# A hybrid token mixer and MLP on one core: the rest of the modulation moved beside the delta rule's inverses

## The chip, the core and the metric

The kernel runs on one NeuronCore of a Trainium2 chip. A core has five engines that matter here, each with its own queue that it works off in order: TensorE (PE; its weight loads are shown apart as PEld), VectorE (DVE), ScalarE (ACT), GpSimd (POOL), and SyncE (SP), which here only issues DMA transfers. ACT and POOL issue some transfers too. Working memory is SBUF (128 partitions); matrix products land in PSUM, eight banks of 128 x 512 floats. The metric is the device time of the whole program in microseconds.

## The reference, cut to what matters

One layer: a token mixer (Hyena long convolution, gated linear attention "GLA", gated delta rule "GDN") and an MLP. Both take shift, scale and gate from a modulation vector, which is a product of SiLU(c), one row, with a matrix of 1024 x 6144.

```python
silu_c = jax.nn.silu(c)
silu_cc = jax.nn.silu(c_ctx)
sh1, sc1, g1, sh2, sc2, g2 = jnp.split((silu_c @ w_mod[l] + b_mod[l])[:, None, :], N_MOD, axis=-1)
csh1, csc1, cg1, csh2, csc2, cg2 = jnp.split(silu_cc @ w_mod[l] + b_mod[l], N_MOD, axis=-1)
h = modulate(x, norm1_g[l], sh1, sc1)
hc = modulate(ctx, norm1_g[l], csh1, csc1)
y, yc = mixer(h, hc, ...)
x = x + g1 * y
x = x + g2 * sq_relu_mlp(modulate(x, norm2_g[l], sh2, sc2), w_mlp1[l], w_mlp2[l])
return rmsnorm(x, final_norm_g)
```

`sh1` and `sc1` are needed before the first projection. The other four parts (`g1`, `sh2`, `sc2`, `g2`) are needed only after the mixer. There are 1024 latent tokens and 256 context tokens.

## The kernel before

The program is written as straight code; a scheduler then sets the order on each engine from the order of writing, from priorities and from its own estimate of times. That order is fixed when the program is built, and on the chip each engine takes its instructions in that order, whatever is ready. A tile belongs to a pool; when a pool is closed, its memory or its PSUM banks go to the next pool on the same side, whose first writer then waits for the last reader of what lay there.

The stages in order:

- Norm, Hyena filters and the first third of the modulation (`mod_group(0)`).
- Input projection: pieces of 128 channels, each 24 products of 128 x 512 per half of the tokens (tiles `psb<-ahi,wh`, `alo,wh`, `ahi,wl`; `ch`, `cl` for the context), weights through `ws`, `wh`, `wl`. Conv pieces are followed by taps on DVE (`acc<-psb,vecs,acc`). Beside the first of them runs the Hyena convolution (tiles `pss`, `hb`, `lv`, `wrh`, `wrl`, `dft`).
- `mod_rest` makes the other two thirds of the modulation. It is a generator; before the change two steps of it are written after each piece of `SEQ[0]`. One group of it (there are two) takes eight row blocks of `wmod`. A row block is 128 rows by 2048 columns of float32, fetched as two halves of 512 KB into the tile `mw` (two buffers). Each half feeds two products with `cs32` (32 columns) as the stationary side. The four products of a row block write four different quarters of 32 partitions of one PSUM bank, `psd`. At the end of a group, ACT copies the bank to SBUF (L452), PE transposes it in four pieces and DVE adds the bias into `modT`.
- `gdn_prep` makes the matrices of the delta rule for four heads (tiles `psp`, `dm`, `KQ`).
- `inverse` inverts triangular matrices for the delta rule: 15 substitution steps in blocks of 16 with the constant selector `sel` (1 MB in SBUF) as the stationary side, then products of 32 x 32 and of 64 x 64 blocks (all in `psi`). Two generators run in `rounds`; every fourth round one gate piece or one decay of `SEQ[2]` is written between.
- `gla_pair`, twice: seven levels of products `pss<-bd,lv` (the last two `bd,kT`), then states. `gdn_loops`: ten steps for four heads (tiles `psl`; a step reads `kv`, `kq`, `at`, its products are `psl<-S,kq`, `r,NT`, `vn,kv`, `vn,at`). The first reads `kv,NT`. `gdn_loops` and the pairs overlap.
- Output projection, MLP, final norm. These read `modT` again.

The pool `psm` (one bank) and the pool `mw` lie on the right side; so do `ia` (the inverse's SBUF, with `sel`), `psi`, and later `nl` and `psl` of `gdn_loops`.

Of the kernel before, what the change touches and what calls it, by code (L numbers as in the profile page):

```python
# [7 lines left out]
F32 = mybir.dt.float32  # L8
# [11 lines left out]
LC = L + CTX  # L20
# [165 lines left out]
EVERY = 4  # L186
ENG = {'eqf': 'vvvvvpvvvvppvv', 'eqr': 'vvvvvvvvvvvvvv', 'qh0': 'vvvvvvvvvvvvvv', 'qh1': 'pppppppppppppp', 'ekf': 'pppppppppppppp', 'ekr': 'vvpppppppppppp', 'kk': 'vvvvvvvvvpvvvv', 'qd0': 'aa', 'qd1': 'aa', 'A': 'vvaa', 'te': 'vvvv', 'ke': 'vvvv', 'kt': 'aaaa', 'A2': 'pppppppppppppppp', 'q2': 'vpvpvpvp', 'og': 'aaaaaaaa', 'ov': 'vv', 'mid': 'paa', 'pk': 'vvvv', 'pq': 'pvpp', 'tri': 'pppppppppppppppp', 'KQ': 'aaaaaaaaaaaaaaaaaaaa', 'C': 'avavavavavavavav', 'off': 'pppp', 'Y': 'pppp', 'T32': 'pppp', 'Ya': 'vvvvvvvvvvvvvvvvvvvvvvvvvvvvvv', 'V': 'aaaa', 'V64': 'aaaa', 'pu': 'aavvaavvaavvaavv', 'NT': 'avavavavavavavavavavavavavavavav', 'Yh': 'vvvvvvvvvvvvvvvv', 'V128': 'aaaaaaaa', 'sp1': 'pppppppppppppppp', 'sp0': 'vvvvvvvvvvvvvvvv', 'spc': 'vvvvvvvvvvvvvvvv', 'sps': 'vvvvvvvvvvvvvvvv', 'wl': 'vvvvvvvvvvvvvvvv', 'yg': 'vvvvvvvv', 'Sl': 'vvvvvvvvvvvvvvvv', 'ft': 'vvvvvvvvvvvvvvvv', 'oq': 'pvpp', 'qs': 'aaaaaaaa', 'S2': 'aaaaaaaa', 'pl': 'vvpvvpvv', 'xr': 'vpvvvvvv', 'kd': 'pppppppp', 'u': 'aaaa'}
ENGC = {'eqf': 'vp', 'eqr': 'vp', 'qh0': 'vp', 'qh1': 'vp', 'ekf': 'vp', 'ekr': 'vp', 'kk': 'vp', 'qd0': 'avp', 'qd1': 'avp', 'A': 'va', 'te': 'vp', 'ke': 'vp', 'kt': 'va', 'A2': 'pva', 'q2': 'vp', 'og': 'va', 'ov': 'vp', 'mid': 'pva', 'pk': 'vp', 'pq': 'vp', 'tri': 'vp', 'KQ': 'va', 'C': 'avp', 'off': 'vp', 'Y': 'pva', 'T32': 'pva', 'Ya': 'vp', 'V': 'va', 'V64': 'va', 'pu': 'va', 'NT': 'avp', 'Yh': 'avp', 'V128': 'va', 'sp1': 'vp', 'sp0': 'vp', 'spc': 'vp', 'sps': 'vp', 'wl': 'vp', 'yg': 'vp', 'Sl': 'vp', 'ft': 'vp', 'oq': 'vp', 'qs': 'av', 'S2': 'avp', 'pl': 'vp', 'xr': 'vp', 'kd': 'vp', 'u': 'av'}
SEQ = ('gk1 gv0 dk0 dq0 gk0 dk1 dv2 gv1 dq1 dk2 gq0 dq2', '0 1 2 dv0 gq1 3 dv1 gv2', 'dg1 0 gg1 gg0 dg0 3 1 gg2 2 dg2')
MODN = 2  # L190
FPOOL = ((0, 2, 5), (0, 2, 5))
# [20 lines left out]
class Build:  # L212
# [99 lines left out]
    def run(self):  # L312
        tc, nc = self.tc, self.nc
        self._cst, self.y, self.nT, self.nS, self.rooms = {}, [], 0, 0, {i: i - 9 for i in range(4)}
        with ExitStack() as es:
# [12 lines left out]
            def tp(name, bufs, right=False, **k):  # L328
                p = tc.tile_pool(reuse_waits="tile", name=name, bufs=bufs, side="right" if right else "left", **k)
                return p, p.__enter__()  # L330
# [23 lines left out]
            close(p0)  # L354
            h, mw = tp("hy", 1, True), tp("mw", 2, True)
            self.H = h[1]
            self.hyena()
            mods = self.mod_rest(psm[1], mw[1])
            piece = lambda n: (self.gdn_conv if n[0] == "d" else self.gla_piece)(n)
            for n_ in SEQ[0].split():  # L360
                piece(n_)
                for _ in range(MODN):
                    next(mods, None)
            for _ in mods:
                pass
            close(mw, h, psm, pss, lv)

# [9 lines left out]

            ia, ib, psi = tp("ia", 1, True), tp("ib", 1, True), ps("psi", 2, True)
            self.inverse_start(ia[1])
            dw = tp("dw", 1, True)  # L380
            dec = self.gla_decays(dw[1])
            rest = [dec[int(n)] if n.isdigit() else (lambda n=n: (self.gate_piece if n[1] == "g" else piece)(n)) for n in SEQ[2].split()]
            self.rounds([self.inverse([X[2 * i + j]["NT"] for j in range(2)], (ia, ib)[i][1], psi[1], f"psi{i}") for i in range(2)], rest, EVERY)
            close(psi, dw, ib, ia)
            close(psb, cv, w, act)
# [53 lines left out]
    def mod_group(self, g, psum, pname, wpool, wnames):  # L439

        nc = self.nc
        ps = psum.tile([128, 512], F32, name=pname)
        for kt in range(8):
            for hf in range(2):
                w = wpool.tile([128, 1024], F32, name=wnames[hf])
                nc.sync.dma_start(w, self.I["wmod"][g, kt, hf])
                for q2 in range(2):
                    q = 2 * hf + q2
                    self.mm(ps[32 * q:32 * q + 32, :], self.cs32[:, kt, :], w[:, 512 * q2:512 * q2 + 512], kt == 0, kt == 7)
            yield  # L450
        ms = wpool.tile([128, 1024], F32, name=wnames[0])[:, :512]
        nc.scalar.copy(ms, ps)  # L452
        pt = psum.tile([128, 512], F32, name=pname)
        for s in range(4):
            self.transpose(pt[:, 128 * s:128 * s + 128], ms[:, 128 * s:128 * s + 128])
        src = pt.rearrange("p (s q c) -> p s q c", s=4, q=4)
        o, _ = _VC["bmod"]
        for col in range(2 if g == 0 else 1):
            self.tt(self.modT[:, 16 * g:16 * g + 16, col].rearrange("p (q s) -> p s q", q=4), src[:, :, :, col],
                    self.vecs[:, o + 16 * g:o + 16 * g + 16].rearrange("p (q s) -> p s q", q=4), ADD)  # L460
        yield

    def mod_rest(self, psum, pool):

        for g in (1, 2):
            yield from self.mod_group(g, psum, "psd", pool, ("mw", "mw"))
        self.stt(self.A2, self.modT[:, 32:40, 0], 1.0, self.vec("n2"), ADD, MUL)
        for g in (20, 44):
            self.ts(self.modT[:, g:g + 4, 0], self.modT[:, g:g + 4, 0], -1.0, MUL)
        self.show("modT", self.modT)  # L470
        yield
# [257 lines left out]
    def gla_decays(self, P):  # L729

        nc, x = self.nc, {}
        wa2 = self.cs32.rearrange("p a b -> p (a b)").rearrange("p (a b) -> p a b", a=2)[:48]

        def start():
            nc.sync.dma_start(wa2, self.I["wa2"])
            ab, smask = x["ab"], x["smask"] = P.tile([48, LC], F32, name="ab"), P.tile([128, LC], F32, name="smask")
            for d in range(2):
                nc.sync.dma_start(ab[32 * d:32 * d + 16], self.dz["gk0"][48 + 64 * d:64 + 64 * d])
            nc.gpsimd.memset(smask, 1.0)
            nc.gpsimd.memset(smask.rearrange("p (a b) -> p a b", b=64)[:, :, 0:1], 0.0)  # L740

        def one(p, d):
# [12 lines left out]
            st = 1 - 2 * d  # L755
            nc.vector.tensor_tensor_scan(t[:, ::st], x["smask"], g[:, ::st], 0.0, op0=MUL, op1=ADD)
            nc.sync.dma_start(self.dcum[p][d], t)
# [289 lines left out]

    def rounds(self, gens, fill=(), every=1):

        n, fill = 0, list(fill)  # L1050
        while gens:
            gens = [g for g in gens if next(g, self) is not self]
            n += 1
            if fill and n % every == 0:
                fill.pop(0)()
        for f in fill:
            f()

    def gdn_loops(self, X):
# [743 lines left out]
```

## Time and profile before

| | |
|---|---|
| median of 3 runs | 1643.51 us (1642.14 to 1655.13) |
| the profiled execution | 1638.78 us |
| its span in the trace | 1637.0 us |
| PE busy | 1509.1 us, 92% of the span |
| DVE busy | 1236.8 us, 76% |
| ACT busy | 803.0 us, 49% |
| POOL busy | 694.8 us, 42% |

The trace is of one execution; 1.8 us of that execution lie outside the span. Times of the trace count from the start of the span. A busy share is an average over stages, so each stage is looked at by itself: the rows further down give stretches of the span, with what each engine did in them.

### The profile page before, as it was taken

Reading aid. Unit: us, or ns where it says so; the run is one execution under the profiler, and the core shown is the slowest. Engines: PE = TensorE matmul, PEld = TensorE weight load, DVE = VectorE, ACT = ScalarE, POOL = GpSimd, SP = SyncE. Lnnn points to the kernel's source line nnn. Section 1 sums busy time; section 2 is a strip of 40 time slices with the busy share of each in tenths; the row PEclk is TensorE's granted clock in tenths of the full one; section 3 lists DMA queues with packets and bytes.
Section 4 is the critical chain, followed back from the end, with each engine's and each line's share of the span. In section 5 each row is a group of like instructions: output and inputs, shape, how many; then the busy total and the mean of one; then the engine's idle time right before and its main releaser. Section 6 shows DMA issues by size and latency. Waiting matters only on the chain.

```text
span 1637.0 us, 26134 instructions
## 1 busy us (share of the span) xinstructions
PE 1509.1 (92%) x10096; PEld 1215.9 (74%) x10096; DVE 1236.8 (76%) x1827; ACT 803.0 (49%) x1462; POOL 694.8 (42%) x494
## 2 busy tenths in 40 slices
PE   7799999989899898758799799999999999999996
PEld 2378877767688676557788687788888888888886
DVE  5963589897576387688887978987679758974995
ACT  5432222315655644445565356654565456446553
POOL 0311141331434330154762354655556555655553
PEclk9899999999999997778889899999999999999998
DMA  8432777756566531136436934364454535453532
GB/s 296 135 110 90 248 258 273 230 188 203 161 211 201 164 135 46 66 118 185 139 112 208 306 103 105 102 155 129 105 140 116 155 83 150 103 142 94 133 70 104
DMA packets 114292, 248.42 MB, mean 152 GB/s; under 512 B 28919, under 2 KB 74407, under 8 KB 101240
## 3 DMA queue, kind: packets, MB, share of 16 engines
q1 hardware_dynamic: 85800, 167.03, 30.3%
q0 software_dynamic: 9808, 59.77, 16.3%
q10 hardware_dynamic: 18560, 19.94, 4.0%
q8 instruction: 80, 1.31, 0.3%
q14 instruction: 44, 0.36, 0.1%
HBM read 196.57 MB, written 41.75 MB: 146 GB/s over the span
## 4 chain that ended last, share of the span: by engine, by line
PE 62%; DVE 22%; ACT 5%; DMA 5%; issue 4%; POOL 2%; SPq 0%; POOLq 0%; ACTq 0%; DVEq 0%
PE psb L224 47%; PE pss L224 8%; DVE lv L252 4%; DVE T L252 3%; PE psl L224 2%; DVE ar L260 2%; DVE hb L252 2%; DVE ar L252 1%; PE psi L224 1%; PE psd L224 1%; DVE acc L260 1%; DVE bd L252 1%; DMA dft<-in_fw 1%; DVE psb L252 1%; DMA alo<-in_xT 1%
## 5 line engine op out<-in xcount | busy, mean ns | idle before, releaser
L224 PE MATMUL psb<-T,S 128*128 128x512 f32 (+1 forms) x3072 | 693.7, 387 | 6.7 <-DVE T L252 3.4
L224 PEld LDWEIGHTS psb<-T,S 128*128 128x128 f32 x3072 | 571.3, 189 | 127.6 <-DVE T L252 5.2
L252 POOL TENSOR_TENSOR S<-wr,S 128x512 fp32r<-128x512 f32 x252 | 366.3, 1468 | 303.4 <-ACT S L292 302.9
L292 ACT CAST S<-wr 128x512 fp32r<-128x512 f32 x252 | 155.0, 620 | 146.9 <-PE psb L224 106.5
L224 PE MATMUL psb<-ahi,wh 128*128 128x512 f32 x448 | 183.5, 411 | 8.5 <-ACT ahi L292 4.3
L224 PE MATMUL psb<-alo,wh 128*128 128x512 f32 x448 | 181.9, 406 | 0.0
L224 PE MATMUL psb<-ahi,wl 128*128 128x512 f32 x448 | 180.6, 403 | 0.0
L252 POOL TENSOR_TENSOR wl<-ws,wh 128x1024 fp32r<-128x1024 f32 x28 | 71.0, 2537 | 208.5 <-ACT wh L292 138.9
L260 DVE SCALAR_TENSOR_TENSOR acc<-psb,vecs,acc 128x504 f32<-128x504 f32 (+5 forms) x168 | 111.2, 677 | 50.4 <-ACT acc L264 48.1
L260 DVE SCALAR_TENSOR_TENSOR x<-psb,modT,x 128x512 f32<-128x512 f32 (+1 forms) x148 | 105.2, 727 | 40.4 <-PE psb L224 40.0
L252 DVE TENSOR_TENSOR T<-h,T 128x512 fp32r<-128x512 f32 x88 | 86.2, 1010 | 46.1 <-ACT T L292 44.8
L224 PEld LDWEIGHTS psb<-ahi,wh 128*128 128x128 f32 x448 | 87.1, 195 | 39.6 <-issue 9.1
L252 DVE TENSOR_TENSOR T<-ar,T 128x512 fp32r<-128x512 f32 x112 | 111.7, 1024 | 6.2 <-ACT T L292 5.9
L224 PEld LDWEIGHTS psb<-alo,wh 128*128 128x128 f32 x448 | 87.1, 195 | 25.7 <-issue 8.0
L224 PEld LDWEIGHTS psb<-ahi,wl 128*128 128x128 f32 x448 | 87.1, 194 | 22.3 <-issue 5.1
L292 ACT CAST T<-ar 128x512 fp32r<-128x512 f32 x112 | 68.5, 620 | 43.8 <-DVE ar L260 29.3
L252 POOL TENSOR_TENSOR bd<-lv,qT 64x1024 f32<-64x1024 f32 x16 | 49.2, 3082 | 37.3 <-PE pss L224 25.1
L264 ACT ACTIVATE acc<-psb,vecs 128x512 f32<-128x512 f32 (+1 forms) x48 | 31.1, 663 | 62.6 <-PE psb L224 29.8
L292 ACT CAST T<-h 128x512 fp32r<-128x512 f32 x88 | 52.3, 618 | 15.9 <-DVE h L260 11.3
L264 ACT ACT_TABLE_LOAD x27 | 34.6, 1283 | 37.5 <-DVE acc L260 17.2
L1774 ACT COPY ar<-psb 128x512 f32<-128x512 f32 x48 | 28.2, 587 | 49.8 <-PE psb L224 49.3
L292 ACT CAST wh<-ws 128x1024 fp32r<-128x1024 f32 x28 | 29.3, 1045 | 44.4 <-PE psb L224 35.1
(335 smaller groups left out, 2663.5 us busy)
## 6 DMA issues: line engine op xcount, KB each, us to landing
wr<-in_w SPq DMA_DIRECT2D x40, 1024.0 KB, 4.9
wr<-in_w POOLq DMA_DIRECT2D x24, 1024.0 KB, 8.0
mw<-in_wmod SPq DMA_DIRECT2D x32, 512.0 KB, 5.1
ws<-in_win SPq DMA_DIRECT2D x28, 512.0 KB, 4.2
dft<-in_fw POOLq DMA_DIRECT2D x8, 1024.0 KB, 5.7
dft<-in_iv POOLq DMA_DIRECT2D x8, 1024.0 KB, 6.0
wr<-wr POOLq DMA_DIRECT2D x8, 1024.0 KB, 7.4
kq<-dKQ SPq DMA_DIRECT2D x64, 96.0 KB, 2.8
```

The source lines that it names most:

```text
L224: return self.nc.tensor.matmul(out, lhsT=lhsT, rhs=rhs, start=start, stop=stop, skip_group_check=more)
L252: return (eng or self.nc.vector).tensor_tensor(out, a, b, op)
L260: return (eng or self.nc.vector).scalar_tensor_tensor(out, a, s, b, op0=op0, op1=op1)
L264: return self.nc.scalar.activation(out, a, f, bias=bias, scale=scale)
L292: self.nc.scalar.copy(hi, src)
L1774: nc.scalar.copy(b[at[i]], ps)
```

## The change

`mod_rest` is no longer stepped between the pieces of `SEQ[0]`. It is handed to `rounds`, which steps it once a round from round 30 on (`MODS_AT`; the 15 substitution steps take 30 rounds), and to its end after the last round. A row block is now one load of 1 MB and four products in a row. Its tile takes the name, and so the single buffer, of the selector `sel` in `ia`; the copy of the finished bank takes that buffer too. The PSUM bank is a pool of its own, `psx`, on the right side under `psi`. The decays' small weights `wa2` get a tile of their own instead of lying over `cs32`, which is now read later; to make room the scan's mask `smask` is halved, and each of the four scans is done in two halves of 640.

```diff
-MODN = 2
+MODS_AT = 30
...
-            h, mw = tp("hy", 1, True), tp("mw", 2, True)
+            h = tp("hy", 1, True)
             self.H = h[1]
             self.hyena()
-            mods = self.mod_rest(psm[1], mw[1])
             piece = lambda n: (self.gdn_conv if n[0] == "d" else self.gla_piece)(n)
             for n_ in SEQ[0].split():
                 piece(n_)
-                for _ in range(MODN):
-                    next(mods, None)
-            for _ in mods:
-                pass
-            close(mw, h, psm, pss, lv)
+            close(h, psm, pss, lv)
...
-            ia, ib, psi = tp("ia", 1, True), tp("ib", 1, True), ps("psi", 2, True)
+            ia, ib, psx, psi = tp("ia", 1, True), tp("ib", 1, True), ps("psx", 1, True), ps("psi", 2, True)
...
-            self.rounds([self.inverse([X[2 * i + j]["NT"] for j in range(2)], (ia, ib)[i][1], psi[1], f"psi{i}") for i in range(2)], rest, EVERY)
-            close(psi, dw, ib, ia)
+            self.rounds([self.inverse([X[2 * i + j]["NT"] for j in range(2)], (ia, ib)[i][1], psi[1], f"psi{i}") for i in range(2)], rest, EVERY,
+                        MODS_AT, self.mod_rest(psx[1], ia[1], "sel"))
+            close(psi, psx, dw, ib, ia)
...
         for kt in range(8):
+            if len(wnames) == 1:
+
+                w = wpool.tile([128, 2048], F32, name=wnames[0])
+                nc.sync.dma_start(w.rearrange("p (h c) -> p h c", h=2), self.I["wmod"][g, kt].rearrange("h p c -> p h c"))
+                for q in range(4):
+                    self.mm(ps[32 * q:32 * q + 32, :], self.cs32[:, kt, :], w[:, 512 * q:512 * q + 512], kt == 0, kt == 7)
+                yield
+                continue
...
-            yield from self.mod_group(g, psum, "psd", pool, ("mw", "mw"))
+            yield from self.mod_group(g, psum, "psd", pool, (name,))
...
-        wa2 = self.cs32.rearrange("p a b -> p (a b)").rearrange("p (a b) -> p a b", a=2)[:48]
+        half = LC // 2
+        wa2 = P.tile([48, 2, 128], F32, name="wa2")
...
-            nc.vector.tensor_tensor_scan(t[:, ::st], x["smask"], g[:, ::st], 0.0, op0=MUL, op1=ADD)
+            for o in range(2):
+                c = slice(half * o, half * o + half)
+                nc.vector.tensor_tensor_scan(t[:, c][:, ::st], x["smask"], g[:, c][:, ::st], 0.0, op0=MUL, op1=ADD)
...
-    def rounds(self, gens, fill=(), every=1):
+    def rounds(self, gens, fill, every, late, other):
...
             if fill and n % every == 0:
                 fill.pop(0)()
+            if n >= late:
+                next(other, None)
         for f in fill:
             f()
+        for _ in other:
+            pass
```

Three places in the built order. First, PE in the middle of the Hyena convolution, where its transposes of `y` stand beside a projection piece. Before:

```order
L224 MATMUL psb<-ahi_940,wh 128x512
L224 MATMUL psb<-alo_941,wh 128x512
L224 MATMUL psb<-ahi_940,wl 128x512
L287 MATMUL pss<-ident,y_1381 128x128 x3
L224 MATMUL psd<-mw,cs_153 32x512 x2
L287 MATMUL pss<-ident,y_1382 128x128
```

With the change:

```order
L225 MATMUL psb<-ahi_970,wl 128x512
L225 MATMUL psb<-ahi_935,wh 128x512
L288 MATMUL psd<-ident,acc 128x128 x4
L288 MATMUL pss<-ident,y_1378 128x128 x3
L225 MATMUL psb<-alo_936,wh 128x512
L288 MATMUL pss<-ident,y_1379 128x128
```

The pair of modulation products is gone from between the Hyena transposes, and products of the projection stand nearer to them.

Second, SP's queue from the end of the gate pieces to the first loads of `gla_pair` (`dz` and `dcum` are stores of gate pieces and decays; `gmask`, `kT`, `qT`, `cum`, `vt` are the first pair's loads; `kq` are the loads of `gdn_loops`). Before:

```order
L757 DMA dcum_105<-acc 128x1280
L688 DMA dz_gg_72<-acc 128x1024
L757 DMA dcum_106<-acc 128x1280
L688 DMA dz_dg_75<-acc 128x1024
L724 DMA gmask<-in_gmask 128x224
L724 DMA kT<-dz_gk_82 128x1280
L724 DMA qT<-dz_gq_84 128x1024
L768 DMA cum<-dcum_104 128x1280
```

With the change:

```order
L444 DMA sel<-in_wmod 128x2x1024 x5
L765 DMA dcum_106<-acc 128x1280
L444 DMA sel<-in_wmod 128x2x1024 x2
L693 DMA dz_dg_75<-acc 128x1024
L729 DMA gmask<-in_gmask 128x224
L729 DMA kT<-dz_gk_82 128x1280
...
L823 DMA vt<-dvt 128x10x192
L444 DMA sel<-in_wmod 128x2x1024
L729 DMA qT<-dz_gq_85 128x1024
L444 DMA sel<-in_wmod 128x2x1024 x7
L1150 DMA kq_7604<-dKQ_98 96x128
```

Eight loads of `wmod` (the first of them stands just ahead of the rows shown) now precede the first pair's loads, and the other eight precede the first `kq`.

Third, PE around the first products of `gdn_loops` (`psl<-kv,NT`). Before:

```order
L224 MATMUL pss<-bd_6288,lv 32x2x32 x27
L224 MATMUL pss<-bd_6287,lv 32x2x32 x32
L224 MATMUL psl<-kv,NT_3539 128x96
L224 MATMUL psl<-kv,NT_3540 128x96
L224 MATMUL psl<-kv,NT_3541 128x96
```

With the change:

```order
L225 MATMUL psd<-sel,cs_153 32x512 x4
L225 MATMUL pss<-bd_6261,kT 32x2x32 x8
L225 MATMUL pss<-bd_6260,kT 32x2x32 x32
L288 MATMUL pss<-ident,lv 128x128 x10
L225 MATMUL psd<-sel,cs_153 32x512 x4
L288 MATMUL psd<-ident,sel 128x128 x4
L288 MATMUL pss<-ident,lv 128x128 x10
L225 MATMUL pss<-vt,lv 64x96 x10
L225 MATMUL psl<-kv,NT_3386 128x96
```

Before, the loops start among the first pair's third and fourth levels. With the change they stand behind all seven levels and behind the last transposes of the modulation. Of its sixteen groups of four products, eight stand among the inverses' products ahead of the first group's transposes, three more among the last 64 x 64 products, and five among the first pair's levels.

## Rows read from the trace of the kernel before

**Rows 1.** The page's 40 slices: PE's busy tenths and its granted clock.

```profile
PE   7799999989899898758799799999999999999996
...
PEclk9899999999999997778889899999999999999998
```

**Rows 2.** Stretches: length, busy us of PE, PEld, DVE, ACT, POOL, clock, DMA.

```profile
192.00:365.00 173.00, 162.53 (x931) 126.53 (x930) 144.62 (x231) 45.87 (x75) 55.47 (x40) 0.97 0.73 252
365.00:430.00 65.00, 64.24 (x347) 46.65 (x347) 46.15 (x78) 31.94 (x48) 21.34 (x15) 1.00 0.67 209
...
500.00:573.00 73.00, 66.93 (x338) 54.30 (x337) 35.75 (x71) 40.89 (x76) 29.52 (x16) 0.98 0.62 189
...
646.00:700.00 54.00, 40.88 (x1426) 33.84 (x1425) 34.20 (x74) 29.35 (x51) 9.34 (x11) 0.72 0.26 92
...
728.00:760.00 32.00, 21.89 (x468) 19.80 (x462) 26.43 (x35) 14.43 (x31) 19.73 (x13) 0.75 0.58 167
```

**Rows 3.** Tile mw alone in two stretches: length, PE, PEld, ACT, clock, DMA.

```profile
192.00:365.00 173.00, 23.84 (x92) 3.59 (x92) 0.59 (x1) 0.97 0.73 252
365.00:430.00 65.00, 10.14 (x44) 1.73 (x44) 0.59 (x1) 1.00 0.67 209
```

**Rows 4.** Timeline: modulation products on PE; start, length; two records are one product.

```profile
211.74 1.07 PE L224 MATMUL psd<-mw,cs 128*32 128x512 f32 x8
...
281.83 1.05 PE L224 MATMUL psd<-mw,cs 128*32 128x512 f32 x4
...
356.36 1.92 PE L224 MATMUL psd<-mw,cs 128*32 128x512 f32 x4
```

**Rows 5.** Shorter stretches of the Hyena stage, columns as in the second group.

```profile
192.00:220.00 28.00, 27.47 (x182) 24.31 (x181) 13.84 (x17) 8.16 (x14) 11.36 (x9) 1.00 0.95 339
...
320.00:340.00 20.00, 17.56 (x115) 14.89 (x114) 20.00 (x32) 4.78 (x8) 12.16 (x7) 1.00 0.85 288
340.00:360.00 20.00, 15.34 (x75) 10.12 (x73) 20.00 (x37) 4.38 (x7) 4.21 (x2) 0.83 0.43 143
```

**Rows 6.** DMA issues: queue, count, KB each, median us from issue to landing.

```profile
wr<-in_w SPq DMA_DIRECT2D x40, 1024.0 KB, 4.9
...
ws<-in_win SPq DMA_DIRECT2D x28, 512.0 KB, 4.2
...
kv<-dtok_v ACTq DMA_DIRECT2D x20, 192.0 KB, 2.9
```

**Rows 7.** Timeline: the selector's last products, and SP's first loads for GLA.

```profile
645.42 0.96 PE L224 MATMUL psi<-i,sel 128*128 128x20 f32 x8
...
689.31 0.38 SPq L724 DMA_DIRECT2D gmask<-in_gmask  x1
...
691.16 2.41 SPq L768 DMA_DIRECT2D cum<-dcum  x2
```

**Rows 8.** Timeline of PE from the first to the last products of the loops.

```profile
730.62 1.88 PE L224 MATMUL psl<-kv,NT 128*128 128x96 f32 x12
...
755.51 1.95 PE L224 MATMUL psl<-r,NT 128*128 128x96 f32 x16
757.30 1.18 PE L224 MATMUL psl<-vn,kv 128*96 128x96 f32 x12
758.49 1.31 PE L287 MATMUL pss<-ident,lv 128*128 128x128 f32 x10
...
889.95 1.09 PE L287 MATMUL pss<-ident,A 128*128 128x128 f32 x8 [0.38 <-ACT A L237]
...
901.34 1.95 PE L224 MATMUL psl<-vn,at 128*128 128x96 f32 x16
```

**Rows 9.** Tiles: engine, operation, count, ns min/median/max, first and last start.

```profile
L452 ACT COPY mw<-psd x2: 586/588/590, 303.2 to 424.0; 128x512 f32<-128x512 f32 x2
...
L756 DVE TENSOR_TENSOR_SCAN acc<-smask,acc x4: 2816/2824/2825, 571.0 to 677.9; 128x1280 f32<-128x1280 f32 x4
...
L252 DVE TENSOR_TENSOR ds<-modT x1: 152/152/152, 914.3 to 914.3; 128x4 f32<-128x4 f32 x1
```

More of the change, by code (lines that the diff above doesn't have):

```diff
@@ L450, in mod_group @@
             yield
-        ms = wpool.tile([128, 1024], F32, name=wnames[0])[:, :512]
+        ms = wpool.tile([128, 2048 // len(wnames)], F32, name=wnames[0])[:, :512]
         nc.scalar.copy(ms, ps)
@@ L461, in mod_group, with mod_rest @@
         yield
-    def mod_rest(self, psum, pool):
+    def mod_rest(self, psum, pool, name):
         for g in (1, 2):
-            yield from self.mod_group(g, psum, "psd", pool, ("mw", "mw"))
+            yield from self.mod_group(g, psum, "psd", pool, (name,))
         self.stt(self.A2, self.modT[:, 32:40, 0], 1.0, self.vec("n2"), ADD, MUL)
@@ L731, in gla_decays @@
         nc, x = self.nc, {}
-        wa2 = self.cs32.rearrange("p a b -> p (a b)").rearrange("p (a b) -> p a b", a=2)[:48]
+        half = LC // 2
+        wa2 = P.tile([48, 2, 128], F32, name="wa2")
         def start():
             nc.sync.dma_start(wa2, self.I["wa2"])
-            ab, smask = x["ab"], x["smask"] = P.tile([48, LC], F32, name="ab"), P.tile([128, LC], F32, name="smask")
+            ab, smask = x["ab"], x["smask"] = P.tile([48, LC], F32, name="ab"), P.tile([128, half], F32, name="smask")
             for d in range(2):
```

## The prediction

> **What bounds the kernel now.** I read the slices first: PE shows 8 or 9 tenths almost everywhere, with one hole in slices 16 to 18, where the clock also falls to 7 and 8 tenths [rows 1]. That hole is the end of the inverses and the start of GLA (646 to 760 us). Then the stretches. While the modulation is made, PE is busy 162.5 of 173 us to the end of Hyena (365 us) and 64.2 of 65 us after it; in the rest of the projection 66.9 of 73 [rows 2]. So PE bounds the projection, but not alone: from 320 to 360 us DVE is busy 40 of 40 us and PE 32.9 of 40 [rows 5]. In the hole nothing is full: PE 40.9 of 54 us (646 to 700), 21.9 of 32 (728 to 760) [rows 2]. These are short dependent products, where a chain of latencies sets the time. The change takes work from a stage where PE is dear and puts it where PE is cheap. The question is whether it brings its own chain.
>
> **What leaves the projection.** 64 products and 8 transposes leave PE: 23.8 us before 365 us and 10.1 after it, 34.0 in all [rows 3]. After 365 us PE has 0.8 us of slack in 65 [rows 2], and DVE only 46 of 65, so I count the 10.1 in full. Before 365 us DVE is next: it is busy 144.6 of 173 us [rows 2], and it loses nothing but two short additions, so its work can at most be pushed together by its idle 28.4 us. Half of that (14.2 us) lies in the first 28 us, where DVE waits for Hyena's beginning and the DMA engines run at 0.95 share [rows 5]; there the modulation's loads leave the queue, which may give a few microseconds, but PE's products do not hold DVE up. That leaves some 14 us of idle time elsewhere as the most that DVE allows there, and nothing as the least, if it is all spent waiting on Hyena's own chain. I take 10: most of PE's relief is of use between the Hyena stretches, little of it where DVE is full. **Gain: 10 + 10 = 20 us**, between 10 (only the part after Hyena) and 34 (all of PE's time).
>
> **What arrives beside the inverses.** Sixteen row blocks. The products themselves get cheaper: a pair from one half took 1.05 us, and the one time that both halves stood together eight records took 1.07 us, since the four quarters of the bank run side by side [rows 4]. At the low level of the clock a pair took 1.92 us [rows 4]; the mean granted clock from 646 to 700 us was 0.72 [rows 2], between the two levels of 1.2 and 2.4 GHz, so I take 1.5 us for a row block, bounds 1.07 and 1.95. That is 24 us of PE in a stage that has 13 us free in its first 54 and 10 in the 32 after 728. But PE's time is not what counts. The tile has one buffer: a load waits for the products of the block before, and they wait for the load. The chain goes like this.
>
> - It can begin when the selector is read for the last time: 645.42 + 0.96 = 646.4 us [rows 7].
> - A 1 MB load from SP lands after 4.9 us; a half of 512 KB took 4.2 [rows 6]. With 1.5 us of products and 0.1 for the hand-overs the period is 6.5 us; sixteen make 104 us. The bounds are 6.1 us (products at 1.07) and 7.0 us (at 1.95).
> - PE takes the groups in its fixed order, so some loads land before PE gets there. The first four groups stand among 32 x 32 products that run quickly, there PE waits for the load instead. For the next four I allow 6 us of loads that wait for PE; between 0 and 12.
> - Between the two groups of eight, and after the last, ACT copies the bank through the same buffer (0.59 us [rows 9]) and PE transposes it: 2 us each time with hand-overs.
>
> The last transposes end near 646.4 + 104 + 6 + 4 = 760 us. `modT` itself is not wanted before 914.3 us [rows 9]. What is wanted is the memory: the loops' `psl` banks and their `kv` tiles come after the chain in PE's and ACT's order, on the side where `psx` and `ia` lay. A `kv` load takes 2.9 us [rows 6], two of them are issued one behind the other; ACT must first get to them. So the loops begin at about **766 us** on the old time scale (before the gain), where they began at 730.6 [rows 8]. The 6 us between are the two loads and ACT's way to them. The bounds: 6.1 us of period and no waiting for PE give 754; 7.0 us and 12 us of waiting give 780.
>
> SP's queue is passed too: `gmask`, `kT`, `qT` and `cum` of the first pair were issued from 689.3 and 691.2 us [rows 7]; now eight loads stand before them, and the eighth cannot be issued before seven periods and PE's waits have passed, 646.4 + 45 + 6 = 698 us or so. GLA then starts some 9 us later, and PE's groups 12 to 16 stand among its levels, so that it also waits for the chain. It reaches the end of its levels at about the same 766 us.
>
> **What the late loops cost.** Not 35 us. At 766 us all seven levels of the first pair are done. Before, this state was reached at 758.49 + 1.31 = 759.8 us [rows 8], and the loops then were one step and most of a second ahead: nine PE rows of `psl` from 730.62 to 757.30 us, 11.4 us together [rows 8]. This work is still to be done. From 759.8 to the end of the loops at 901.34 + 1.95 = 903.3 us there were 143.5 us [rows 8], with PE and DVE both largely busy, so I add the 11.4 in full: 766 + 143.5 + 11.4 = 920.9 us. **Loss: 17.6 us.** A second reading agrees in size: in the new order the second pair's last transposes come about one step of the loops sooner, so more of the loops runs alone at the end; alone, from 889.95 to 903.3 us, a step took about 13 us [rows 8]. With the start at 754 or 780 us the loss is 6 or 32 us.
>
> **Small things.** The four scans of 2.82 us [rows 9] become eight of half the length. The extra fixed parts lie on DVE beside the inverses; I put 0.4 us of them in the range and none in the sum. The `wa2` load leaves the place where it waited for the modulation to end. The late consumers see nothing, since `modT` comes more than 100 us ahead of need. These I cost at nothing, covered by the chain above.
>
> **Sum.** -20 + 17.6 = -2.4 us. On the profiled execution's 1638.78 us that is 1636.4. It ran 4.7 us under the median of the runs shown, 1643.51, to which the forecast is carried: **1641 us**. The extreme sums are -34 + 6 = -28 and -10 + 32 = +22 us.
>
> **A rule against the trace.** The rows give 4.9 us for 1 MB. The Trainium skill, "DMA: Bandwidth & Descriptors", section "Anatomy of one DMA — SWDGE (gpsimd) path", fits a transfer as about 2 us fixed plus bytes over 436 GB/s, an estimate of 4.4 us here; by it the sixteen loads would be 8 us shorter and the sum -10 us, about 1633. The fit is for the other kind of queue than SP's, so the row decides.
>
> **Rivals.**
>
> *The projection gives back nearly all, and the chain is short (faster).* If Hyena is held by PE's order rather than by DVE, 30 of the 34 us come back; if the period is near 6.1 us with little waiting for PE, the loops begin near 756 us and the loss is 8. Sum -22: 1621 us. For it: PE was 94% busy before 365 us, and the DMA engines, at 0.73 share there [rows 2], lose 16 MB of loads. Against it: DVE's full 40 us, and the low clock in the receiving stage.
>
> *The single buffer decides (slower).* The ring of load and products holds PSUM and SBUF that the loops need; every microsecond more in its period costs 16 us at the loops' start. Gain and loss meet at a period of 6.65 us; from 7.7 us on the kernel is over 1% slower. At 7.9 us the loops start 22 us later still, and the sum is -20 + 40 = +20: 1663 us. Such a period comes if the loads share the DMA engines with GLA's loads or the products run at the low clock throughout with PE late. For it: half the chain is in a stage at clock 0.72 and below. Against it: DMA was only at 0.26 share there [rows 2]. The Trainium skill says as a general rule "Double-buffer for performance: Overlap DMA with compute" ("Trainium Kernel Development and Optimization", "Best Practices"); this ring does not, and the rule speaks for this rival. No row shows such a ring yet.
>
> *The loops aren't held (inside the forecast).* If they could start before the modulation ends, only GLA's later loads would count, 9 us: sum -11, 1632 us. PE's and ACT's order speak against it.
>
> **How the numbers follow.** A measurement of this kernel can tell about 1%, 16 us. The forecast with what lies within 1% of no change (1627 to 1660) gets 0.58; the faster rival, with everything below 1627, 0.26; the slower, above 1660, 0.16. The range goes from the faster rival's time to just short of the slower one's, 1620 to 1661, and so holds the forecast and about half of each rival: some 0.21 is left out. The extreme sums, 1616 and 1666, lie a few microseconds beyond it on both sides.
>
> **What would show it.** In the new trace: the old window of 192 to 430 us should be done about 20 us earlier, with DVE near full in Hyena (right), or 30 earlier (first rival). `wmod` loads should be issued 6 to 7 us apart from about 626 us on the new scale, 16 of them, with PE products `psd<-sel` of 1 to 2 us for eight records. `psl<-kv,NT` should come about 35 us later against the selector's end than before (120 us after it instead of 84), and the end of the loops about 17 us later against it. I would be wrong if the projection is not shorter by at least 10 us, if the period is outside 6.0 to 7.2 us, or if the scheduler's new order costs or gives time in places that I have not looked at: the heads of `gdn_prep`, and the second pair beside the loops.

## The result: slower by 3%, and the profile after

| | before | after |
|---|---|---|
| median | 1642.96 us (4 runs, 1642.14 to 1655.13) | 1698.07 us (4 runs, 1693.77 to 1707.18) |
| ratio to before | | 1.0315, 95% interval 1.0279 to 1.0352 |
| the profiled execution | 1638.78 us | 1707.18 us |
| its span | 1637.0 us | 1705.4 us |

The forecast was 1641 us, with a range of 1620 to 1661. The profiled execution is 68.4 us longer than that of before; the medians are 55.1 us apart, and the other 13.3 us lie in which executions were traced (that of before ran 4.2 us under its median, this one 9.1 us above its own). The page's slices of the changed kernel, which answer to [rows 1], show where: PE's hole is wider, and a new, shallower one stands in slices 6 to 11, where the modulation's products were taken out.

```profile
PE   7799988877799887756889599999999999999997
...
PEclk9899999978899978877879789999999999999998
```

The stretches, in the columns of [rows 2], with the same landmarks (Hyena's last products start at 369.2 instead of 367.5 us, the selector's last product starts at 651.9 instead of 646.1):

```profile
192.00:369.00 177.00, 149.63 (x877) 134.75 (x876) 150.09 (x241) 47.92 (x78) 61.85 (x39) 0.89 0.51 174
369.00:430.00 61.00, 44.74 (x242) 37.33 (x241) 40.58 (x55) 26.86 (x42) 20.04 (x12) 0.86 0.50 150
...
652.00:700.00 48.00, 33.35 (x1053) 20.68 (x1054) 26.54 (x59) 20.31 (x34) 4.54 (x6) 0.82 0.43 146
...
730.00:760.00 30.00, 15.11 (x320) 10.33 (x320) 15.31 (x17) 6.26 (x14) 5.77 (x4) 0.73 0.37 122
760.00:800.00 40.00, 21.77 (x404) 15.24 (x404) 29.53 (x26) 14.96 (x18) 25.49 (x18) 0.65 0.36 127
```

The first two lines are the first surprise. PE is now idle for 27 of 177 us and for 16 of 61, where it had 10 and 1 [rows 2]; the stage did not get shorter by any of it. The selector ends 5.8 us *later* than before. The DMA share fell from 0.73 to 0.51, so the loads are gone too. DVE is busy for 150 of the 177 us where it was for 145 of 173. What PE waits for from 192 to 369 us (in total, times, longest us):

```profile
PE pss L225 <- DVE wrl L253: 9.5, 2, 4.8
PE psb L225 <- DVE acc L261: 8.0, 1, 8.0
PE pss L225 <- ACT wrh L293: 5.2, 2, 5.1
PE pss L225 <- DVE y L261: 4.7, 1, 4.7
```

Of PE's 27 us of idle time, 22.2 end with DVE. Before, up to 365 us, PE waited 3.1 us for `wrl` and 2.4 for `y`, and not at all for the taps (`acc`).

The second surprise is the length of the ring. The timeline of PE, from the first group of modulation products to the last, and on to the first product of the loops (start, length; eight records are one row block; in brackets the idle time before and what ended it):

```profile
658.94 1.07 PE L225 MATMUL psd<-sel,cs 128*32 128x512 f32 x8
659.93 2.19 PE L225 MATMUL psi<-i,i 32*32 32x32 f32 x226
665.09 1.65 PE L225 MATMUL psd<-sel,cs 128*32 128x512 f32 x8 [2.96 <-DMA sel<-in_wmod]
...
679.59 1.93 PE L225 MATMUL psd<-sel,cs 128*32 128x512 f32 x8 [3.11 <-DMA sel<-in_wmod]
...
706.90 1.06 PE L225 MATMUL psd<-sel,cs 128*32 128x512 f32 x8 [1.35 <-DMA sel<-in_wmod]
...
713.01 1.06 PE L225 MATMUL psd<-sel,cs 128*32 128x512 f32 x8 [1.45 <-DMA sel<-in_wmod]
...
727.92 1.06 PE L225 MATMUL psd<-sel,cs 128*32 128x512 f32 x8 [0.26 <-DMA sel<-in_wmod]
...
739.06 3.32 PE L225 MATMUL psi<-i,NT 64*64 64x64 f32 x52 [8.56 <-DVE NT L1349]
742.31 1.85 PE L225 MATMUL psd<-sel,cs 128*32 128x512 f32 x8
...
749.14 1.07 PE L225 MATMUL psd<-sel,cs 128*32 128x512 f32 x8 [2.62 <-DMA sel<-in_wmod]
...
751.22 0.86 PE L225 MATMUL pss<-bd,lv 128*32 128x64 f32 x44
...
791.78 1.94 PE L225 MATMUL psd<-sel,cs 128*32 128x512 f32 x8 [4.16 <-DMA sel<-in_wmod]
...
794.42 1.12 PE L288 MATMUL psd<-ident,sel 128*128 128x128 f32 x4 [0.71 <-ACT sel L457]
...
799.01 1.13 PE L225 MATMUL psl<-kv,NT 128*128 128x96 f32 x8
```

Read it in two ways. Where a group has a bracket with `DMA sel`, PE came first and stood: 19.2 us in nine waits from 640 to 800 us. Where it has none, as at 742.31, the load had landed and stood waiting for PE, which was held by something else; there it was 8.56 us for DVE's copy of `NT`. Both kinds of waiting lie on the one chain. The sixteen loads are issued from 652.1 to 785.3 us, 8.9 us apart in the mean, and the loops begin at 799.0 us, 147 us after the selector instead of 84 [rows 7, 8].

SP's queue, with the lines that answer to those of [rows 7]; a line of several issues shows the time from the first to the last:

```profile
652.14 0.39 SPq L444 DMA_DIRECT2D sel<-in_wmod  x1
...
699.74 8.66 SPq L444 DMA_DIRECT2D sel<-in_wmod  x2
710.45 0.34 SPq L693 DMA_DIRECT2D dz_dg<-acc  x1
710.84 0.44 SPq L729 DMA_DIRECT2D gmask<-in_gmask  x1
...
713.99 0.93 SPq L776 DMA_DIRECT2D cum<-dcum  x2
...
729.05 56.64 SPq L444 DMA_DIRECT2D sel<-in_wmod  x7
```

`gmask` comes 59 us after the selector instead of 43, and the first level of GLA on PE 99 us after it (751.22) instead of 65. Before, that level began here:

```profile
710.92 1.94 PE L224 MATMUL pss<-bd,lv 128*32 128x64 f32 x64 [7.39 <-DVE lv L252]
```

From the start of the loops to their last product it takes 178.0 us (799.0 to 977.0) where it took 172.4; one stall of that is new, `at` landing late behind loads of the next stage, which now start while the loops still run:

```profile
974.54 2.85 PE L225 MATMUL psl<-vn,at 128*128 128x96 f32 x12 [12.62 <-DMA at<-dAT]
```

So the 68.4 us are: selector +5.8, selector to loops +62.6, the loops +5.6, and the rest −5.6.

### The profile page after: what moved, and what is told of

It is laid out like the page before. It is cut to its first block, busy times and chain, and to the rows that moved or that the text cites. A ratio compares the mean times of both kernels' runs of the same rounds, so it can differ in the third digit from the quotient of the medians.

```text
span 1705.4 us, 26111 instructions
## 1 busy us (share of the span) xinstructions
PE 1514.2 (89%) x10096; PEld 1233.5 (72%) x10096; DVE 1247.3 (73%) x1831; ACT 800.1 (47%) x1461; POOL 704.2 (41%) x494
## 5 line engine op out<-in xcount | busy, mean ns | idle before, releaser
L253 POOL TENSOR_TENSOR wl<-ws,wh 128x1024 fp32r<-128x1024 f32 x28 | 79.4, 2837 | 221.2 <-ACT wh L293 170.7
L253 DVE TENSOR_TENSOR T<-h,T 128x512 fp32r<-128x512 f32 x88 | 92.9, 1086 | 44.6 <-ACT T L293 43.3
L253 DVE TENSOR_TENSOR T<-ar,T 128x512 fp32r<-128x512 f32 x112 | 108.2, 994 | 6.8 <-ACT T L293 6.5
L293 ACT CAST T<-ar 128x512 fp32r<-128x512 f32 x112 | 68.4, 620 | 46.1 <-DVE ar L261 31.0
L293 ACT CAST wh<-ws 128x1024 fp32r<-128x1024 f32 x28 | 29.3, 1047 | 55.1 <-PE psb L225 41.2
```

What stands on the lines that cost most here:

```text
L253: return (eng or self.nc.vector).tensor_tensor(out, a, b, op)
L293: self.nc.scalar.copy(hi, src)
```

## The experiments

The question falls in two: why the projection gave nothing back, and what made the loops so late. Each kernel was timed beside the kernel before on the same chip (its median there 1645 to 1649 us).

### What the products were worth in the projection

**`e1_no_mod`** leaves the rest of the modulation out altogether (`modT` and `A2` are constants); everything else is the changed kernel.

```diff
-                        MODS_AT, self.mod_rest(psx[1], ia[1], "sel"))
+                        MODS_AT, iter(()))
```

> The changed kernel with the other two thirds of the modulation left out altogether (modT and A2 are filled with constants), so nothing of it is beside the inverses either. Theory F (filler): before the change the modulation's products on PE filled gaps that Hyena's DVE chain and the decays' chain leave, so taking them away gains nothing; the selector's last products end at 641 to 652 us as before (646), the whole takes 1632 to 1648 us, and all of the 55 us between the two kernels is the price of the row blocks beside the inverses. Rival P (PE bounds the projection, as I had counted): the selector's end comes 15 to 30 us earlier and the whole takes 1612 to 1628 us; then the price beside the inverses is 70 to 85 us.

Measured: 1645.86 us, ratio 0.9992 (0.9966 to 1.0018). With 34 us of PE and 16 MB of loads taken away and nothing put elsewhere, the kernel is not faster. Up to the selector's end (652.0 us) its trace is nearly that of the changed kernel: PE busy 149.15 of 177 us and 44.90 of 61. So the gain is missing in the projection itself, and is not eaten up later. Selector to loops is 82.6 us: all of the 62.6 us of delay belongs to the modulation beside the inverses.

**`e2_small_parts`** is the kernel before with only the halved scans and the tile for `wa2`.

```diff
-            nc.vector.tensor_tensor_scan(t[:, ::st], x["smask"], g[:, ::st], 0.0, op0=MUL, op1=ADD)
+            for o in range(2):
+                c = slice(half * o, half * o + half)
+                nc.vector.tensor_tensor_scan(t[:, c][:, ::st], x["smask"], g[:, c][:, ::st], 0.0, op0=MUL, op1=ADD)
```

> The kernel before with only the small parts of the change: the scan's mask halved and each scan in two halves, and wa2 in a tile of its own. Theory F: no difference, 1638 to 1648 us. Rival: these parts, with the other order that they bring, cost part of the 55 us, 1653 us or more.

Measured: 1647.68 us, ratio 0.9991 (0.9967 to 1.0014). Nothing, as the prediction had it. But its trace moves the landmark: the selector's last product starts at 650.9 us, with the modulation still in its old place. So 4.8 of the 5.8 us by which it is late in the changed kernel need not come from the modulation; the small parts, their order or the execution that was traced give as much. Against this kernel, leaving the modulation out (`e1_no_mod`, second line) moves the selector by 1.1 us (count, shortest, median and longest in ns, first and last start):

```profile
L224 PE MATMUL psi<-i,sel x120: 173/282/617, 595.7 to 650.9; 128*128 128x300 f32 x8, 128*128 128x280 f32 x8, 128*128 128x260 f32 x8, 128*128 128x240 f32 x8
...
L225 PE MATMUL psi<-i,sel x120: 182/283/602, 596.4 to 652.0; 128*128 128x300 f32 x8, 128*128 128x280 f32 x8, 128*128 128x260 f32 x8, 128*128 128x240 f32 x8
```

In the changed kernel the eight scans take 1.475 us each, 0.5 us more in all than the four of [rows 9].

**`e3_one_load_old_place`** keeps the modulation where it was before and only fetches a row block in one load, into one buffer.

```diff
-            h, mw = tp("hy", 1, True), tp("mw", 2, True)
+            h, mw = tp("hy", 1, True), tp("mw", 1, True)
...
-            yield from self.mod_group(g, psum, "psd", pool, ("mw", "mw"))
+            yield from self.mod_group(g, psum, "psd", pool, ("mw",))
```

> The kernel before, modulation in its old place, but a row block in one load with four products in a row, and one buffer of 1 MB instead of two of 512 KB. PE loses some 15 us of work in the projection (32 pairs at 1.0 us become 16 fours at 1.07). Theory F: no gain, 1636 to 1650 us. Rival P: 1625 to 1634 us. A third case, that the single buffer makes a slow ring here too and the modulation ends late: over 1655 us.

Measured: 1642.21 us, ratio 0.9952 (0.9920 to 0.9983). The products and transposes of the rest of the modulation take 18.8 us of PE there instead of 34.0 [rows 3]; a record lasts 0.617 us in the median. This part of the change is a small gain, and this kernel is the fastest complete version here. That halving the products gives a little more than leaving them out (`e1_no_mod`) is not explained by any theory here; the built order differs all over the projection, and how much of these few microseconds is the order's is not shown.

**`e7_before_few_taps` and `e8_no_mod_few_taps`** take the other engine away: in the kernel before, and in `e1_no_mod`, four of the six side taps of the delta rule's convolutions are left out.

```diff
-                if o:
+                if o and (taps == 3 or abs(o) == 1):
```

> The kernel before, with four of the six side taps of each convolution of the delta rule left out (two thirds of DVE's scalar_tensor_tensor work on acc there; the output is not the layer's). It takes some 20 us off DVE between 192 and 369 us and as much again before 577 us. Theory D (in the projection PE bounds the kernel before, and DVE takes its place as soon as PE is relieved): here PE still bounds, so little is gained: 1640 to 1648 us against 1648 for before. Rival C (chains of latencies in Hyena and in the decays bound the stage, neither engine): within 4 us of before here too. Rival B (DVE bounds already before): 1635 us or less.

> The kernel with the rest of the modulation left out entirely, and with the same four of six side taps left out. Against the 1645.9 us that it took with all taps: theory D (PE relieved of 34 us, DVE is what holds the projection): with DVE relieved as well, the first products of the delta rule's matrices come at least 12 us earlier than 430 us, and the time is 1634 us or less. Rival C (chains of latencies bound the stage, neither engine): 1640 to 1648 us, the first of those products still near 430 us.

Measured, as ratios to the kernel before:

| | all taps | few taps |
|---|---|---|
| with the modulation in the projection | 1 | 0.9953 (0.9930 to 0.9975) |
| without it | 0.9992 (0.9966 to 1.0018) | 0.9862 (0.9834 to 0.9890) |

DVE's work on `acc` from 192 to 577 us falls from 100.4 to 38.2 us in the first row. Alone that is worth 0.5%. The modulation's PE time alone is worth nothing. Together they are worth 1.4%, and with few taps the relief of PE is worth 15 us (1638.87 to 1623.56). This is the core of theory D: two engines bound the projection together, and relief of one shows the other.

The modulation's loads go together with its products in this step, but they were hardly waited for: in `e7_before_few_taps` PE waits 1.6 us for loads of any kind from 192 to 430 us.

Two figures of the expectations failed. The time of `e7_before_few_taps` (1638.87 us) lies outside all three ranges, 1 us below that of theory D. And the first products of the delta rule's matrices do not come earlier in `e8_no_mod_few_taps` (436.5 us); the scheduler put other pieces ahead of them. The gain lies further on. Hyena's last products start at 367.5 us before and 369.2 with the change, at 355.6 in `e7_before_few_taps` and 353.2 in `e8_no_mod_few_taps`: its end follows the taps, and PE's relief moves it by some 2 us either way. From 367 to 577 us PE is busy 205.3 of 210 us in `e7_before_few_taps`, and there the relief shows: the matrices' last products (`psp<-KQ`) start at 561.0 instead of 590.5 us, and the selector's last product at 628.5 instead of 654.5 us (652.0 in `e1_no_mod`). Each of these kernels is built anew with an order of its own; no run holds the order fixed, so what part of the missing gain is the order's stays open.

The stretches of `e8_no_mod_few_taps`, cut at its own end of Hyena, in the columns of [rows 2]:

```profile
192.00:353.00 161.00, 149.58 (x910) 134.00 (x909) 128.65 (x207) 48.85 (x81) 65.01 (x39) 0.97 0.57 194
353.00:430.00 77.00, 67.22 (x344) 56.21 (x344) 38.03 (x53) 45.07 (x82) 30.80 (x21) 0.93 0.52 148
```

PE is busy for the same 149.6 us within 161 us where it was within 177 us with all taps, and its granted clock is at 0.97 instead of 0.89. The wait of 8.0 us for `acc` is gone from this stretch; that for `wrl` (9.2 us) is still there.

### What made the loops late

**`e6_one_load_per_group`** is the changed kernel with fourteen of the sixteen loads left out; all products stay, most of them on the data of the first load of their group.

```diff
-                w = wpool.tile([128, 2048], F32, name=wnames[0])
-                nc.sync.dma_start(w.rearrange("p (h c) -> p h c", h=2), self.I["wmod"][g, kt].rearrange("h p c -> p h c"))
+                if kt == 0:
+                    w = wpool.tile([128, 2048], F32, name=wnames[0])
+                    nc.sync.dma_start(w.rearrange("p (h c) -> p h c", h=2), self.I["wmod"][g, kt].rearrange("h p c -> p h c"))
```

> The changed kernel with 14 of the 16 loads left out: one load for each of the two groups, and all eight groups of four products read it, so the modulation's values are wrong. Theory L (the round trip of load and products through one buffer holds the loops): the loops' first products come 85 to 105 us after the selector's end instead of 147, and the whole takes 1645 to 1660 us. Rival O (PE's fixed order and the resources held, not the loads, make the delay): the loops still begin 125 us or more after the selector's end and the whole takes 1680 us or more.

Measured: 1670.39 us, ratio 1.0109 (1.0040 to 1.0178). The loops begin 96 us after the selector, within theory L's range; the time lies between the two theories. Of the loss between `e1_no_mod` and the changed kernel, 28 of 52 us go with the loads by the medians, 34 of 53 by the ratios; the four runs of this kernel lie between 1658 and 1679 us, so half to two thirds is as close as this gets. The rest stays with the products alone. So a group of products between two steps of a chain of 32 x 32 products is not free, though PE was idle there by the average: in the order on PE the chain stands behind it. One wait that follows shows in the trace: PE stands 7.0 us for DVE's copy of `NT`, as for 8.56 us in the changed kernel, where in `e1_no_mod` it stands 2.3.

**`e4_two_half_buffers`** gives the ring two buffers of 512 KB (the selector in two tiles).

```diff
-            yield from self.mod_group(g, psum, "psd", pool, (name,))
+            yield from self.mod_group(g, psum, "psd", pool, (name + "0", name + "1"))
```

> The changed kernel, with the selector in two tiles of half the size, so that the two halves of a row block have a buffer each and a half's load can run beside the other half's products. Theory L (the ring of load and products through one buffer is what holds the loops back): a row block then takes the 4.2 us of a half's load and about 1 us of products where PE comes at once, 5.3 us instead of 6.1 to 7.5, some 20 us less over sixteen; the loops begin 115 to 132 us after the selector's last product instead of 147, and the time falls to 1670 to 1688 us. Rival O (PE's fixed order, in which the groups stand among products that are late for reasons of their own): the loads still wait for PE, the loops still begin 140 us or more after the selector, and the time stays at 1690 us or above.

Measured: 1700.68 us, ratio 1.0345 (1.0302 to 1.0388). The ring does get shorter, as theory L said: the loops begin 124 us after the selector instead of 147. The time does not follow; it lies in rival O's range. GLA's first level comes later, at 760.8 us, behind fifteen of the sixteen row blocks' products on PE where it stood behind eleven, and the end of the loops follows GLA. Its line (count, shortest, median and longest in ns, first and last start):

```profile
L225 PE MATMUL pss<-bd,lv x640: 216/314/316, 760.8 to 889.4; 128*32 128x64 f32 x160
```

**`e9_ring_on_pool_queue`** issues the loads of the row blocks from POOL's queue, so that SP's is free for GLA.

```diff
-                nc.sync.dma_start(w.rearrange("p (h c) -> p h c", h=2), self.I["wmod"][g, kt].rearrange("h p c -> p h c"))
+                nc.gpsimd.dma_start(w.rearrange("p (h c) -> p h c", h=2), self.I["wmod"][g, kt].rearrange("h p c -> p h c"))
```

> The changed kernel, with the sixteen row-block loads issued from POOL's queue instead of SP's, so that GLA's first loads no longer stand behind eight of them. Theory L (the ring itself): GLA's mask is issued near 697 us instead of 711, but PE's groups and the last transposes still follow the ring; the loops begin 135 to 150 us after the selector's last product, time 1683 to 1700 us. Rival Q (what costs is SP's queue, in which GLA's loads wait for the ring): the first levels begin near 720 us and the loops no more than 115 us after the selector; time 1675 us or less.

Measured: 1723.03 us, ratio 1.0477 (1.0434 to 1.0520): outside both theories, on L's side. SP's queue, in the columns as above, was not what held GLA:

```profile
699.77 0.32 SPq L765 DMA_DIRECT2D dcum<-acc  x1
713.47 0.32 SPq L693 DMA_DIRECT2D dz_dg<-acc  x1
713.84 0.42 SPq L729 DMA_DIRECT2D gmask<-in_gmask  x1
```

No row block stands in front of `gmask`, and it still comes at 713.84, right behind the store of the last gate piece. That piece's products stand behind the groups on PE. The extra 25 us go with a longer ring: POOL reaches the last loads only between its own work for GLA (the last is issued at 798.6 us), and the loops begin at 825.0. POOL itself now stands before these loads until PE has read the tile, 59.5 us in nine waits, so for the time, other than for `gmask`, this run is no clean test of SP's queue.

**`e10_one_group_each`** leaves the first group in the projection and puts only the second beside the inverses.

```diff
+            mods = self.mod_group(1, psm[1], "psd", mw[1], ("mw",))
...
-        for g in (1, 2):
+        for g in (2,):
```

> The changed kernel, with the first of the two groups of the rest of the modulation back in the input projection (eight 1 MB loads, one buffer) and only the second beside the inverses. Theory L with the loss in proportion to the ring's length: eight row blocks of 7.5 us end near 715 us, before GLA's levels; the loops begin 85 to 102 us after the selector's last product, time 1648 to 1664 us. Rival H (the ring costs mainly by being there, with its pools held to the end of the inverses): the loops begin 120 us or more after it, time above 1675 us. Rival P (PE's time in the projection is dear after all): half of its relief shows, time under 1640 us.

Measured: 1658.11 us, ratio 1.0088 (1.0054 to 1.0123), within theory L's range; the loops begin 97 us after the selector. Half the ring costs a little over a quarter of the loss, since it ends at 707 us, before GLA's levels; GLA's first level is late there too, by 25 us against `e1_no_mod`.

**`e13_ring_behind_inverses`** writes all sixteen row blocks behind the last round.

```diff
-MODS_AT = 30
+MODS_AT = 999
```

> The changed kernel with the sixteen row blocks written behind the last round (MODS_AT 999 instead of 30): the built order then has no group of products between the inverses' products of 32 x 32, one load stands ahead of GLA's first loads on SP's queue instead of eight, and fifteen groups stand among GLA's levels and states. Theory M (two holds in one change: groups between the inverses delay the last gate piece and so GLA, and the ring's end holds the memory of the loops; the later of the two decides): inverses and gate piece run as without the modulation, GLA's first level comes 68 to 78 us after the selector's last product as there (69), but the loops begin 165 to 205 us after it, and the time is 1720 to 1760 us. Rival I (the groups between the inverses are what costs, and loops that begin late are made up for by running beside less of GLA): 1690 us or less.

Measured: 1729.18 us, ratio 1.0505 (1.0463 to 1.0547), as theory M said. Without groups among the inverses' 32 x 32 products, `gmask` comes 45 us after the selector, the same as in `e1_no_mod`; GLA's first level comes after 80.5 us, a little over the 78 expected (two groups still stand ahead of it). But the loops, which come behind the ring, begin 202 us after it. Its lines, in the columns of the line of `e4_two_half_buffers`:

```profile
L225 PE MATMUL psd<-sel,cs x128: 589/1060/1062, 714.2 to 844.9; 128*32 128x512 f32 x128
...
L225 PE MATMUL psl<-kv,NT x16: 248/275/350, 853.7 to 857.9; 128*128 128x96 f32 x16
...
L225 PE MATMUL psl<-vn,at x128: 248/275/529, 896.1 to 994.1; 128*128 128x96 f32 x128
```

All kernels with all taps side by side, in us after the start of the selector's last product. These landmarks are of one traced execution each; the last column is the median of the runs:

| | `gmask` issued | first level of GLA | loops begin | last product of the loops | time, us |
|---|---|---|---|---|---|
| before | 43.2 | 64.8 | 84.5 | 256.9 | 1643 |
| `e1_no_mod` | 45.0 | 68.6 | 82.6 | 254.6 | 1646 |
| `e2_small_parts` | 43.9 | 65.6 | 79.7 | 259.0 | 1648 |
| `e3_one_load_old_place` | 42.6 | 64.1 | 79.9 | 269.3 | 1642 |
| `e10_one_group_each` | 57.4 | 93.5 | 97.1 | 277.4 | 1658 |
| `e6_one_load_per_group` | 53.8 | 91.6 | 95.6 | 281.1 | 1670 |
| after | 58.9 | 99.3 | 147.1 | 325.1 | 1698 |
| `e4_two_half_buffers` | 65.3 | 112.5 | 124.4 | 309.3 | 1701 |
| `e9_ring_on_pool_queue` | 63.8 | 107.5 | 175.0 | 340.6 | 1723 |
| `e13_ring_behind_inverses` | 45.0 | 80.5 | 202.4 | 342.8 | 1729 |

Where the loops begin up to 20 us behind GLA's first level, their end comes 184 to 205 us after that level. Where they begin later, it follows their own start by 140 to 178 us. Two things go with the time, GLA's start and the moment when the loops may begin, and the ring delays both: early groups the first, late groups the second. No place of the whole ring that was tried spares both. Whether the loops wait for the ring's memory or for their place behind it in the fixed order was not separated; in the changed kernel, in `e9_ring_on_pool_queue` and in `e13_ring_behind_inverses` their first load of `kv` is issued within 0.2 us of the end of the last row block's products.

## Why the prediction was wrong

**What held.** The ring's parts: a load landed after 4.9 us in the median; where PE was on time the period was 6.1 to 7.5 us (658.94 to 665.09, 706.90 to 713.01), about the 6.5 forecast. Groups of four products took 1.06 to 1.96 us. The loops wait for the ring's last transposes and begin about 4 us after them, and the last transposes of GLA's levels run next to the ring's (795 us), as said. The small parts cost nothing.

**"After 365 us PE has 0.8 us of slack in 65 [rows 2], and DVE only 46 of 65, so I count the 10.1 in full", and 10 of 23.8 before.** This step failed first: a gain of 20 us, not below 10, was forecast; the selector came 5.8 us later (4.8 later in the trace of the small parts alone), and with the modulation left out the kernel took the same time as before. That PE was full did not mean that PE bounded the stage. Much of what filled it stood where PE would otherwise have waited for others. Relieved, PE ran convolution pieces a little earlier, whose taps the code writes with high priority: DVE did 55 of them before Hyena's end instead of 48, 35.2 us instead of 30.9, and Hyena's own DVE work came no earlier. After Hyena, DVE seems to be held by the chain that starts the delta rule's decays (`gdn_rows`) and not by its busy time: it waited 8.7 us for ACT and 6.5 us for a load of `dz_gk` from 369 to 430 us. The runs with and without taps show the coupling; which of these waits is the last one in each place was not taken apart.

**"For the next four I allow 6 us of loads that wait for PE; between 0 and 12", and 2 us for each copy with its transposes.** Against 6.5 us a period, the first eight groups lost 8.6 us, inside these bounds. But from the eighth group to the ninth there were 14.9 us, 8.4 over a period where 2 were allowed; and the last eight, for which nothing was allowed, lost 18.4 (63.86 us for seven periods). The chain had said that these groups stand among GLA's levels, and the sum did not price it. The loops began 62.6 us later against the selector instead of 35.

**"SP's queue is passed too".** GLA started 16 us later against the selector by its mask, and 34.5 by its first level, not 9. The queue was the wrong cause: `e9_ring_on_pool_queue` frees it, and `gmask` comes no earlier. The last gate piece on PE, behind the groups, was late; then the level's work stands on DVE ahead of the copy of `NT` that the second inverse waits for (8.56 us), and the first level stands on PE behind that inverse.

**"Not 35 us."** From 35 us of late start the prediction took 17.8 back, because GLA would be finished when the loops begin, so that the rest runs quicker. That is real, and `e13_ring_behind_inverses` shows it: 140.4 us from the first to the last product instead of 172.4. Here it did not come, because GLA was late as well, and the loops then ran 45 us alone (932 to 977 us) where they had run 13, beside the next stage's loads; 12.6 of the 45 us are the one stall on `at`, which no other trace here has, so part of this may belong to the execution that was traced.

In sum: −2.4 forecast, 25.8 for the gain that is not there, 27.2 for the ring, 23.4 for the credit and the loops themselves, 5.6 back behind them: 68.4, as between the two traces. The slower rival had the right side. It priced a longer period of the ring, over 1% slower from 7.7 us on, and the groups did stand 8.9 us apart in the mean; but the single buffer alone does not decide: two buffers shorten the ring and leave the time where it was, and in the order built for them GLA comes later. The Trainium skill's rule to double-buffer ("Trainium Kernel Development and Optimization", "Best Practices") thus holds for the transfer here (124 us instead of 147 to the loops) and not for the kernel. Its fit for a transfer ("DMA: Bandwidth & Descriptors", "Anatomy of one DMA — SWDGE (gpsimd) path"), made for loads from POOL's queue, gives an estimate of 4.4 us for 1 MB; measured were 4.9 us from SP and 5.4 from POOL, so the row of before was the better guide for the sum.

## What to carry to other kernels

An engine that is busy 95% of a stage need not bound it: before work is moved off it, leave that work out altogether, and see whether the stage gets shorter. Idle time in a chain of short dependent products on an in-order engine is not simply room: a group put there can end up on the chain, with the wait for its load. And a tile or bank that is reused beside such a chain hands its delay on to whoever gets that memory next, or stands next in the order; where two things follow, look at both starts, since a remedy for one can delay the other.

## What was not expected of the hardware

With the modulation out of the projection, PE idles more and its granted clock falls, from 0.97 to 0.89 before Hyena's end and from 1.00 to 0.86 after it, between the levels of 1.2 and 2.4 GHz; with the taps out too it is at 0.97 in the first stretch. What the prediction took from a single row [rows 4] holds for all sixteen row blocks: four products into the four quarters of one bank take about as long as two, 1.06 us in stretches with a granted clock of 1.00 (706.90 us) and 1.94 where it was 0.50 (791.78 us), against 1.05 and 1.92 for two; in the old place that alone saved 15 us of PE (`e3_one_load_old_place`).
